# One 512-column matmul in place of two of 256 in the gate/up product of a two-layer decoder trunk

## The chip, the cores and the metric

The kernel runs on one core of a Trainium2 chip, in one launch. The metric is device time in microseconds (us): 1181.53 us is the median of three timed runs of the kernel before (1181.19 to 1183.71).

## The reference

The input is 256 tokens of 1024 features in float32. Two layers follow each other. Each adds half a SwiGLU, then an attention, then half a second SwiGLU to the residual stream. The attention of the first layer is a dilated-window attention, that of the second a latent attention. So there are four SwiGLUs, each with its own weights:

```python
def swiglu(x, w_in, w_out):
    gate, up = jnp.split(x @ w_in, 2, axis=-1)
    return (jax.nn.silu(gate) * up) @ w_out

x = x + 0.5 * swiglu(rmsnorm(x, norm_gains[i, 0]), ffn_w_in[i, 0], ffn_w_out[i, 0])
...                                   # x = x + attention(rmsnorm(x))
x = x + 0.5 * swiglu(rmsnorm(x, norm_gains[i, 2]), ffn_w_in[i, 1], ffn_w_out[i, 1])
```

The hidden width is 2816, that is 22 chunks of 128. The weights are streamed from HBM in pieces of 1 MB.

## The kernel before

Activations stay on the chip with features on the partitions: `xT[p, kt, token]` holds feature kt*128+p of 256 tokens. A float32 product is made of three passes in a rounded 32-bit format (float32r) over an exact split of both operands into a high and a low part: hi·xh + hi·xl + lo·xh, all accumulated in one PSUM bank. The function `mm3` (line 91) issues the three matmuls (lines 95, 96 and 97). The weight is the stationary operand, so each matmul comes with its own weight load, and the 256 tokens are the moving columns.

A weight piece is loaded by SyncE (line 81) into `raw`, cast to `hi` on ScalarE (line 87), and the rest `lo` is taken on VectorE (line 88). Four raw buffers and three each of `hi` and `lo` rotate: a cast waits until the matmuls that read the piece three before it have ended. The gained activation is split in the same way by `split_x` into the tiles `xh` and `xl` (lines 114 and 115), chunk by chunk, at the end of the stage before.

`ffn` (line 170) is a SwiGLU. For each of the 22 hidden chunks c, `up(c)` multiplies by the gate half and the up half of the weights: for each of 8 feature chunks k and for both halves u one `mm3`, 48 matmuls of 256 columns, into the two halves of one PSUM bank of the pool `wk`. `gate(c)` then multiplies the bank by the inverse root mean square of every token (`bc`, line 195, VectorE), applies Silu to the gate half (line 199, ScalarE), multiplies the halves (line 201, VectorE) and splits the product h into `hh` (line 204, ScalarE) and `hl` (line 205, VectorE). `down(c)` multiplies h by 128 rows of the second weight: 24 matmuls of 256 columns into the four accumulator banks of the pool `acc`. The work runs as up, up, two downs, up, up, two downs, where the downs belong to chunks two and three before. The first three ups have no downs between them, because `bc` is not there yet: `stats` and `spread_rstd` (lines 147 and 158) make it with a few small matmuls in the meantime. The last four downs are closed bank by bank (line 247), and each bank's residual and split feed the next stage.

The engines run in order. The order is set at build time: the framework interleaves the instructions of the program by its own estimate of when operands are ready, so an engine's list does not follow the source line by line. Of the eight PSUM banks `acc` has four, `wk` three and `ob` one, for the whole program.

Of the kernel before, what the change touches and what calls it, by code (L numbers as in the profile page):

```python
"""Two-layer hybrid decoder trunk (dilated-window attention, latent attention) on one core.

Activations stay on chip, feature-major: xT[p, kt, token] holds feature kt*128+p.  Products of
float32 operands against the weights run as three float32r passes over an exact split
w = hi + lo (12 significant bits each): hi*xh + hi*xl + lo*xh.  RMS-norm scales are applied
after the products (per token), so a product never waits for a norm's statistics.

The tokens stand even ones first, then odd ones: a dilation of 4 or 16 never joins the two
halves, so those groups' scores are two diagonal blocks.  Only inside the latent layer are they
in their own order, which its input's split and its output's residual turn to and from.  # L10
"""
# [10 lines left out]
F32 = mybir.dt.float32  # L22
# [3 lines left out]
ALU = mybir.AluOpType  # L26
# [24 lines left out]
class Trunk:  # L51
    def __init__(self, ctx, tc):
# [9 lines left out]
        self.wk = e(tc.tile_pool(name="wk", bufs=3, space=PSUM))  # L62
        self.ob = e(tc.tile_pool(name="ob", bufs=1, space=PSUM))
# [3 lines left out]
        self.xh = self.xp.tile([P, KT, S], F32R, name="xh")  # L67
        self.xl = self.xp.tile([P, KT, S], F32R, name="xl")

    # ---- weights: load a piece, split it exactly into two float32r parts  # L70
    def piece(self, src, cuts=1, before=None):
        """cuts: parts the split is made in; before: called ahead of each part's load, else it's one load."""
# [18 lines left out]
    def mm3(self, out, terms, start, stop, **kw):  # L91
        """out += sum over (wh, wl, xh, xl) of w x; the weight is stationary."""
# [6 lines left out]
    # ---- residual stream  # L99
    def split_x(self, d0, xs, in_order=False, shared=False):  # L100
        """Gained x (chunks from d0) as float32r pairs, with the tokens even|odd or in their own order;
        shared: ScalarE and VectorE take turns at the high parts."""
# [14 lines left out]
    def squares(self, d0, xs, in_order=False):  # L117
        """The sum of squares over the chunks."""
# [16 lines left out]
    def residual(self, d0, n, acc, scale, in_order=False):  # L135
        """x += scale * acc for n chunks from d0; acc is their part of a bank, its tokens maybe in order."""
# [10 lines left out]
    def stats(self):  # L147
        """Per-token mean square + eps and its inverse root."""
        nc = self.nc
        ps = self.ob.tile([P, 512], F32, name="ob")  # L150
# [7 lines left out]
    def spread_rstd(self):  # L158
        """The inverse root along the free axis, on every partition."""
# [4 lines left out]
        ps = self.ob.tile([P, 512], F32, name="ob")  # L164
# [4 lines left out]
    # ---- SwiGLU  # L169
    def ffn(self, up_w, out_w, finish, start=None, started=None, hook=None):  # L170
        nc, tc = self.nc, self.tc
        with tc.tile_pool(name="ff", bufs=2) as ff, tc.tile_pool(name="hh", bufs=6) as hp:
            accs = [self.acc.tile([P, 512], F32, name="acc") for _ in range(4)]
            hs, wos = {}, {}

            def up(c, midway=None):
                hi, lo = self.piece(up_w[c], 4 if c < 6 else 1, start if c == 0 else None)
                hv, lv = (t.rearrange("p (k u c) -> p k u c", k=KT, u=2) for t in (hi, lo))
                ps = self.wk.tile([P, 512], F32, name="wk")
                for k in range(KT):  # L180
                    for u in range(2):
                        self.mm3(
                            ps[:, u * S : (u + 1) * S],
                            [(hv[:, k, u, :], lv[:, k, u, :], self.xh[:, k, :], self.xl[:, k, :])],
                            k == 0 and u == 0,
                            k == KT - 1 and u == 1,
                            skip_group_check=True,
                        )
                    if midway and k == KT // 2:
                        midway()  # L190
                return ps

            def gate(c, ps):
                gu = ff.tile([P, 2, S], F32, name="gu")
# [769 lines left out]
```

## Time and profile before

| what | before |
|---|---|
| timed runs, median (range) | 1181.53 us (1181.19 to 1183.71) |
| span of the profiled execution | 1178.2 us |
| TensorE matmul busy (share of the span) | 1159.9 us (98%) |
| VectorE busy | 792.3 us (67%) |
| ScalarE busy | 593.1 us (50%) |
| DMA moved | 196.59 MB, mean 167 GB/s |
| share of the closing chain, by engine | TensorE 90%, VectorE 6% |
| matmuls | 9142, of them 4224 of the gate/up product |

The page of the profile gives for each engine the time in which at least one of its instructions ran. TensorE's matmuls overlap, so a matmul's own duration (0.28 us) is not what it costs: that is the distance from one start to the next. The chain is followed back from the last instruction, at each step to what released it. The profiled execution's own time is its span; the median of the timed runs is 3.3 us longer.

The four SwiGLUs take the stretches 0 to 202, 496 to 686, 686 to 876 and 984 to 1178 us of the span, roughly; the two attentions lie between.

### The profile page before, as it was taken

Reading aid. Unit: us, or ns where it says so; the run is one execution under the profiler, and the core shown is the slowest. Engines: PE = TensorE matmul, PEld = TensorE weight load, DVE = VectorE, ACT = ScalarE, POOL = GpSimd, SP = SyncE. Lnnn points to the kernel's source line nnn. Section 1 sums busy time; section 2 is a strip of 40 time slices with the busy share of each in tenths; the row PEclk is TensorE's granted clock in tenths of the full one; section 3 lists DMA queues with packets and bytes.
Section 4 is the critical chain, followed back from the end, with each engine's and each line's share of the span. In section 5 each row is a group of like instructions: output and inputs, shape, how many; then the busy total and the mean of one; then the engine's idle time right before and its main releaser. Section 6 shows DMA issues by size and latency. Waiting matters only on the chain.

```text
span 1178.2 us, 21736 instructions
## 1 busy us (share of the span) xinstructions
PE 1159.9 (98%) x9142; PEld 1106.9 (94%) x9142; DVE 792.3 (67%) x1384; ACT 593.1 (50%) x980; POOL 102.6 (9%) x98
## 2 busy tenths in 40 slices
PE   7999999999999999999999999999999899999998
PEld 7999999888888888999999999999998789999998
DVE  6855557979777776675555676555576897655554
ACT  6444445556555555654444454444466875444441
POOL 2000001212111111200000020000013212000000
PEclk9999999999999999999999999999999999999999
DMA  8655554554444344155555545555533235455540
GB/s 319 216 182 191 191 186 144 214 179 144 141 146 144 112 158 142 56 215 179 184 184 189 192 182 179 179 179 183 184 129 122 108 110 184 175 183 191 192 149 37
DMA packets 29042, 196.59 MB, mean 167 GB/s; under 512 B 3344, under 2 KB 3856, under 8 KB 5904
## 3 DMA queue, kind: packets, MB, share of 16 engines
q1 hardware_dynamic: 28944, 195.21, 47.4%
q8 instruction: 71, 1.16, 0.4%
q14 instruction: 27, 0.22, 0.1%
HBM read 194.14 MB, written 1.05 MB: 166 GB/s over the span
## 4 chain that ended last, share of the span: by engine, by line
PE 90%; DVE 6%; ACT 2%; issue 1%; POOL 1%; DMA 1%; SPq 0%; DVEq 0%; POOLq 0%
PE wk L96 14%; PE wk L97 14%; PE wk L95 14%; PE acc L95 9%; PE acc L97 9%; PE acc L96 9%; PE acc L418 3%; PE acc L420 3%; PE acc L419 3%; PE wk L358 1%; PE acc L432 1%; PE acc L434 1%; DVE lo L88 1%; PE acc L433 1%; PE ob L491 1%; PE wk L446 1%
## 5 line engine op out<-in xcount | busy, mean ns | idle before, releaser
L88 DVE TENSOR_TENSOR lo<-raw,hi 128x512 fp32r<-128x512 f32 (+2 forms) x408 | 447.0, 1119 | 213.2 <-ACT hi L87 211.6
L87 ACT CAST hi<-raw 128x512 fp32r<-128x512 f32 (+2 forms) x408 | 375.2, 963 | 277.2 <-PE wk L96 172.9
L95 PE MATMUL wk<-xh,hi 128*128 128x256 f32 x1408 | 399.8, 284 | 1.6 <-ACT hi L87 1.6
L97 PE MATMUL wk<-xh,lo 128*128 128x256 f32 x1408 | 399.0, 283 | 1.8 <-DVE lo L88 1.8
L96 PE MATMUL wk<-xl,hi 128*128 128x256 f32 x1408 | 398.8, 283 | 0.1
L97 PEld LDWEIGHTS wk<-xh,lo 128*128 128x128 f32 x1408 | 269.9, 192 | 2.6 <-DVE lo L88 2.6
L95 PEld LDWEIGHTS wk<-xh,hi 128*128 128x128 f32 x1408 | 270.1, 192 | 2.2 <-ACT hi L87 2.1
L96 PEld LDWEIGHTS wk<-xl,hi 128*128 128x128 f32 x1408 | 270.0, 192 | 0.8 <-DVE xl L115 0.5
L95 PE MATMUL acc<-hh,hi 128*128 128x256 f32 x704 | 197.2, 280 | 0.0
L97 PE MATMUL acc<-hh,lo 128*128 128x256 f32 x704 | 196.4, 279 | 0.0
L96 PE MATMUL acc<-hl,hi 128*128 128x256 f32 x704 | 196.4, 279 | 0.0
L95 PEld LDWEIGHTS acc<-hh,hi 128*128 128x128 f32 x704 | 132.3, 188 | 0.0
L97 PEld LDWEIGHTS acc<-hh,lo 128*128 128x128 f32 x704 | 132.3, 188 | 0.0
L96 PEld LDWEIGHTS acc<-hl,hi 128*128 128x128 f32 x704 | 131.9, 187 | 0.0
L204 ACT CAST hh<-h 128x256 fp32r<-128x256 f32 x88 | 35.4, 406 | 168.2 <-DVE h L201 168.0
L195 DVE TENSOR_TENSOR gu<-wk,bc 128x512 f32<-128x512 f32 x88 | 60.5, 691 | 76.5 <-PE wk L97 76.2
L418 PE MATMUL acc<-hi,xh 128*128 128x512 f32 x192 | 76.6, 399 | 0.0
L419 PE MATMUL acc<-lo,xh 128*128 128x512 f32 x192 | 75.2, 392 | 0.0
L420 PE MATMUL acc<-hi,xl 128*128 128x512 f32 x192 | 74.9, 390 | 0.0
L205 DVE TENSOR_TENSOR hl<-h,hh 128x256 fp32r<-128x256 f32 x88 | 37.1, 424 | 33.2 <-ACT hh L204 33.1
L562 POOL TENSOR_TENSOR rr<-r,mhalf 128x8 f32<-128x8 f32 x24 | 39.2, 1636 | 205.2 <-DVE r L560 205.2
L130 POOL TENSOR_TENSOR ssq<-sq 128x256 f32<-128x256 f32 x6 | 4.8, 796 | 596.3 <-ACT sq L127 422.0
(183 smaller groups left out, 1521.3 us busy)
## 6 DMA issues: line engine op xcount, KB each, us to landing
raw<-in_up SPq DMA_DIRECT2D x87, 1024.0 KB, 4.8
raw<-in_down SPq DMA_DIRECT2D x44, 1024.0 KB, 4.8
raw<-in_a_qk SPq DMA_DIRECT2D x24, 1024.0 KB, 4.8
raw<-in_a_v SPq DMA_DIRECT2D x12, 1024.0 KB, 4.8
raw<-in_a_out SPq DMA_DIRECT2D x4, 1024.0 KB, 5.4
raw<-in_b_out SPq DMA_DIRECT2D x4, 1024.0 KB, 4.9
raw<-in_b_in SPq DMA_DIRECT2D x3, 1024.0 KB, 4.9
raw<-in_b_q SPq DMA_DIRECT2D x4, 576.0 KB, 3.6
```

The lines of the kernel that those rows point to most:

```text
L87: nc.scalar.copy(hi[:, c], raw[:, c])
L88: nc.vector.tensor_tensor(lo[:, c], raw[:, c], hi.bitcast(F32)[:, c], op=ALU.subtract)
L95: self.nc.tensor.matmul(out, wh, xh, start=start and i == 0, stop=False, **kw)
L96: self.nc.tensor.matmul(out, wh, xl, start=False, stop=False, **kw)
L97: self.nc.tensor.matmul(out, wl, xh, start=False, stop=stop and i == n - 1, **kw)
L195: nc.vector.tensor_tensor(gu, ps.rearrange("p (u s) -> p u s", u=2), self.bc.unsqueeze(1).broadcast_to([P, 2, S]), op=ALU.mult)
L204: nc.scalar.copy(hh, h)
L205: nc.vector.tensor_tensor(hl, h, hh.bitcast(F32), op=ALU.subtract)
L418: nc.tensor.matmul(pss[tt], xh, hi[:, k, :], start=kk == 0, stop=False)
L419: nc.tensor.matmul(pss[tt], xh, lo[:, k, :], start=False, stop=False)
L420: nc.tensor.matmul(pss[tt], xl, hi[:, k, :], start=False, stop=kk == KT - 1)
L562: nc.gpsimd.tensor_tensor(rr, r8, self.mhalf[:, :8], op=ALU.pow)
```

## The change

In `up` the two parts of the activation now stand side by side in one tile `xs[p, k, part, token]`. The high weight part meets both of them in one matmul of 512 columns, which fills a whole bank: hi·xh in its first half, hi·xl in its second. The low weight part meets `xh` in a matmul of 256 columns that accumulates onto the first half. Gate and up have a bank each, so a chunk takes two banks. Afterwards ScalarE copies the second halves of both banks into SBUF (`rest`), and VectorE adds them to the first halves (`gu`). `gate` then multiplies `gu` by `bc` in SBUF, where before it read PSUM.

The banks are shared out anew: within a SwiGLU a pool `up` has two buffers of two banks each, and `wk` and `ob` exist only within the attentions. The small matmuls of the statistics go to `acc` banks within a SwiGLU, and the accumulators are taken at the first down. Comments were taken out of the file as well, which shifts its line numbers; they are left out here.

```diff
-        self.wk = e(tc.tile_pool(name="wk", bufs=3, space=PSUM))
-        self.ob = e(tc.tile_pool(name="ob", bufs=1, space=PSUM))
...
-        self.xh = self.xp.tile([P, KT, S], F32R, name="xh")
-        self.xl = self.xp.tile([P, KT, S], F32R, name="xl")
+        self.xs = self.xp.tile([P, KT, 2, S], F32R, name="xs")
+        self.xh, self.xl = self.xs[:, :, 0, :], self.xs[:, :, 1, :]
+
+    def attention_banks(self, ctx):
+        self.wk = ctx.enter_context(self.tc.tile_pool(name="wk", bufs=3, space=PSUM, reuse_waits="tile"))
+        self.ob = ctx.enter_context(self.tc.tile_pool(name="ob", bufs=1, space=PSUM, reuse_waits="tile"))
+        self.small = lambda: self.ob.tile([P, 512], F32, name="ob")
...
+            tc.tile_pool(name="up", bufs=2, space=PSUM, reuse_waits="tile") as up_banks,
+        ):
+            self.small = lambda: self.acc.tile([P, 512], F32, name="acc")
+            accs, hs, wos = [], {}, {}
...
-                ps = self.wk.tile([P, 512], F32, name="wk")
+                ps = up_banks.tile([P, 2, 2, S], F32, name="up")
                 for k in range(KT):
+                    both = self.xs[:, k].rearrange("p t s -> p (t s)")
                     for u in range(2):
-                        self.mm3(
-                            ps[:, u * S : (u + 1) * S],
-                            [(hv[:, k, u, :], lv[:, k, u, :], self.xh[:, k, :], self.xl[:, k, :])],
...
+                        nc.tensor.matmul(
+                            ps[:, u].rearrange("p t s -> p (t s)"), hv[:, k, u, :], both, start=k == 0, stop=False, skip_group_check=True
+                        )
+                        nc.tensor.matmul(
+                            ps[:, u, 0, :], lv[:, k, u, :], self.xh[:, k, :], start=False, stop=k == KT - 1, skip_group_check=True
                         )
...
-                return ps
-
-            def gate(c, ps):
-                gu = ff.tile([P, 2, S], F32, name="gu")
-                nc.vector.tensor_tensor(
-                    gu, ps.rearrange("p (u s) -> p u s", u=2), self.bc.unsqueeze(1).broadcast_to([P, 2, S]), op=ALU.mult
-                )
+                rest = ff.tile([P, 2, S], F32, name="rest")
+                nc.scalar.copy(rest, ps[:, :, 1, :])
+                gu = ff.tile([P, 2, S], F32, name="gu", bufs=4)
+                nc.vector.tensor_tensor(gu, ps[:, :, 0, :], rest, op=ALU.add)
+                return gu
+
+            def gate(c, gu):
+                nc.vector.tensor_tensor(gu, gu, self.bc.unsqueeze(1).broadcast_to([P, 2, S]), op=ALU.mult)
...
             def down(c, ds=range(KT)):
                 hi, lo = wos[c // 2]
+                if not accs:
+                    accs.extend(self.acc.tile([P, 512], F32, name="acc") for _ in range(4))
```

The order of instructions moves at three places that matter below. The first is VectorE at the start of the program, from the statistics of the first SwiGLU (`var`) on. Before:

```order
L154 TENSOR_SCALAR var_260<-ob_257 128x2
L163 TENSOR_SCALAR dg_325<-ident_85,rstd_262 128x128 x2
L88 TENSOR_TENSOR lo_217<-raw_214,hi_216 128x512 x4
L167 COPY bc_330<-ob_328 128x256
L195 TENSOR_TENSOR gu_350<-wk_148,bc_330 128x512
```

Now (L159, L168, L172 and L93 are the old lines 154, 163, 167 and 88; L204 is the new add and L208 the multiplication by `bc`):

```order
L159 TENSOR_SCALAR var_230<-acc_227 128x2
L168 TENSOR_SCALAR dg_283<-ident_78,rstd_232 128x128 x2
L204 TENSOR_TENSOR gu_175<-up_140,rest_173 128x512
L172 COPY bc_288<-acc_286 128x256
L93 TENSOR_TENSOR lo_197<-raw_194,hi_196 128x512 x4
L208 TENSOR_TENSOR gu_175<-gu_175,bc_288 128x512
```

The first chunk's add and the copy of `bc` now stand ahead of the split of the second chunk's weights (`lo_217` before, `lo_197` now).

The second is VectorE in the middle of a SwiGLU, over one period of two ups and two downs. Before, `lo_1208` is a piece of the down weights, and the others are of the gate/up weights:

```order
L88 TENSOR_TENSOR lo_1208<-raw_1205,hi_1207 128x2048
L195 TENSOR_TENSOR gu_1195<-wk_1146,bc_330 128x512
L88 TENSOR_TENSOR lo_1273<-raw_1270,hi_1272 128x2048
L201 TENSOR_TENSOR h_1199<-sg_1197,gu_1195 128x256
L205 TENSOR_TENSOR hl_1202<-h_1199,hh_1201 128x256
L195 TENSOR_TENSOR gu_1260<-wk_1211,bc_330 128x512
```

Now, with `lo_1113` a piece of the down weights:

```order
L93 TENSOR_TENSOR lo_1113<-raw_1110,hi_1112 128x2048
L204 TENSOR_TENSOR gu_1047<-up_1012,rest_1045 128x512
L208 TENSOR_TENSOR gu_1047<-gu_1047,bc_288 128x512
L93 TENSOR_TENSOR lo_1167<-raw_1164,hi_1166 128x2048
L212 TENSOR_TENSOR h_1052<-sg_1050,gu_1047 128x256
L204 TENSOR_TENSOR gu_1099<-up_1064,rest_1097 128x512
L216 TENSOR_TENSOR hl_1055<-h_1052,hh_1054 128x256
L208 TENSOR_TENSOR gu_1099<-gu_1099,bc_288 128x512
```

Each chunk has one VectorE instruction more, the add, and `hl` of a chunk now stands behind the add of the next one.

The third is TensorE at the end of the first SwiGLU, where the last chunk's product h meets the down weights. Before, from the 25th matmul after the last up (`hh_2121` is chunk 20, `hh_2186` chunk 21; `acc_109` is the first accumulator):

```order
L95 MATMUL acc_109<-hh_2121,hi_2192 128x256
L96 MATMUL acc_109<-hl_2122,hi_2192 128x256
L97 MATMUL acc_109<-hh_2121,lo_2193 128x256
L95 MATMUL acc_109<-hh_2121,hi_2192 128x256
L96 MATMUL acc_109<-hl_2122,hi_2192 128x256
L97 MATMUL acc_109<-hh_2121,lo_2193 128x256
L95 MATMUL acc_109<-hh_2186,hi_2192 128x256
L96 MATMUL acc_109<-hl_2187,hi_2192 128x256
```

Now, from the 43rd matmul after the last up (`hh_1896` is chunk 21, `hh_1738` chunk 19; `acc_405` is the third accumulator; L100 to L102 are the old lines 95 to 97):

```order
L100 MATMUL acc_405<-hh_1738,hi_1744 128x256
L101 MATMUL acc_405<-hl_1739,hi_1744 128x256
L100 MATMUL acc_403<-hh_1896,hi_1902 128x256
L100 MATMUL acc_404<-hh_1896,hi_1902 128x256
L102 MATMUL acc_405<-hh_1738,lo_1745 128x256
L100 MATMUL acc_405<-hh_1738,hi_1744 128x256
L101 MATMUL acc_403<-hl_1897,hi_1902 128x256
```

The last chunk's `hh` was needed by the 31st matmul after the last up and is now needed by the 45th; its `hl` by the 32nd and now by the 49th. Matmuls of the third accumulator, which before came after the first two were complete, have moved ahead of them.

## Rows read from the trace of the kernel before

**Rows 1.** The page: busy time by engine, and the closing chain by engine.

```profile
PE 1159.9 (98%) x9142; PEld 1106.9 (94%) x9142; DVE 792.3 (67%) x1384; ACT 593.1 (50%) x980; POOL 102.6 (9%) x98
...
PE 90%; DVE 6%; ACT 2%; issue 1%; POOL 1%; DMA 1%; SPq 0%; DVEq 0%; POOLq 0%
```

**Rows 2.** Busy time inside the four SwiGLUs: stretch, length, PE, PEld, DVE, ACT, POOL.

```profile
512.00:683.00 171.00, 171.00 (x1434) 170.95 (x1434) 101.77 (x110) 74.23 (x89) 0.74 (x1) 1.00 0.54 185
...
sum 646.00, PE 646.00 PEld 645.89 DVE 385.40 ACT 277.35 POOL 3.03; mean PE 161.50 PEld 161.47 DVE 96.35 ACT 69.34 POOL 0.76
```

**Rows 3.** Timeline of TensorE, last up to first down: start, duration, line.

```profile
190.58 0.28 PE L95 MATMUL wk<-xh,hi 128*128 128x256 f32 x1
...
190.94 0.28 PE L95 MATMUL acc<-hh,hi 128*128 128x256 f32 x1
...
191.29 0.28 PE L95 MATMUL acc<-hh,hi 128*128 128x256 f32 x1
```

**Rows 4.** Timeline of TensorE in the dilated attention: matmuls of 512 and 256 columns.

```profile
302.59 0.39 PE L418 MATMUL acc<-hi,xh 128*128 128x512 f32 x1
...
306.22 0.39 PE L419 MATMUL acc<-lo,xh 128*128 128x512 f32 x1
...
219.36 0.40 PE L418 MATMUL acc<-hi,xh 128*128 128x512 f32 x1
219.60 0.40 PE L419 MATMUL acc<-lo,xh 128*128 128x512 f32 x1
...
231.18 0.28 PE L432 MATMUL acc<-hi,xh 128*128 128x256 f32 x1
231.29 0.28 PE L433 MATMUL acc<-lo,xh 128*128 128x256 f32 x1
```

**Rows 5.** Groups by line and shape: busy us, mean ns, idle before.

```profile
L360 ACT COPY pt<-wk 128x512 f32<-128x512 f32 x32 | 18.3, 585 | 10.0 <-PE wk L358 10.0
...
L195 DVE TENSOR_TENSOR gu<-wk,bc 128x512 f32<-128x512 f32 x88 | 60.5, 691 | 76.5 <-PE wk L97 76.2
...
L576 DVE TENSOR_TENSOR t<-t,t 128x512 f32<-128x512 f32 x24 | 16.5, 688 | 0.4
...
L88 DVE TENSOR_TENSOR lo<-raw,hi 128x2048 fp32r<-128x2048 f32 x108 | 247.5, 2292 | 149.6 <-ACT hi L87 149.5
```

**Rows 6.** Timeline at the second chunk of the first SwiGLU: VectorE, then TensorE.

```profile
17.91 0.48 DVE L163 TENSOR_SCALAR dg<-ident,rstd 128x128 f32<-128x128 f32 x2 [0.83 <-POOL rstd L156]
18.31 2.49 DVE L88 TENSOR_TENSOR lo<-raw,hi 128x512 fp32r<-128x512 f32 x4
...
18.54 0.67 PE L165 MATMUL ob<-dg,ones 128*128 128x256 f32 x2 [1.65 <-DVE dg L163]
...
19.28 0.28 PE L97 MATMUL wk<-xh,lo 128*128 128x256 f32 x1
```

**Rows 7.** Timeline at the entry to the second SwiGLU: VectorE, then TensorE.

```profile
499.70 1.83 DVE L115 SCALAR_TENSOR_TENSOR xl<-xg,xh 128x256 fp32r<-128x256 f32 x2
...
500.71 0.39 PE L96 MATMUL wk<-xl,hi 128*128 128x256 f32 x1
...
501.58 0.39 PE L96 MATMUL wk<-xl,hi 128*128 128x256 f32 x1
```

**Rows 8.** Timeline at the end of the first SwiGLU: VectorE, ScalarE, TensorE.

```profile
191.14 0.69 DVE L195 TENSOR_TENSOR gu<-wk,bc 128x512 f32<-128x512 f32 x1 [0.37 <-PE wk L97]
191.75 1.28 DVE L88 TENSOR_TENSOR lo<-raw,hi 128x512 fp32r<-128x512 f32 x2
...
193.89 0.42 DVE L205 TENSOR_TENSOR hl<-h,hh 128x256 fp32r<-128x256 f32 x1
...
191.06 1.14 ACT L87 CAST hi<-raw 128x512 fp32r<-128x512 f32 x2 [0.75 <-PE wk L96]
192.11 0.42 ACT L199 ACTIVATE sg<-gu 128x256 f32<-128x256 f32 x1
...
194.47 0.28 PE L95 MATMUL acc<-hh,hi 128*128 128x256 f32 x1
```

More of the change, by code (lines that the diff above doesn't have):

```diff
@@ L149, in stats @@
         nc = self.nc
-        ps = self.ob.tile([P, 512], F32, name="ob")
+        ps = self.small()
         for tt in range(NTT):
@@ L163, in spread_rstd @@
             nc.vector.tensor_scalar(dg[:, tt, :], self.ident, self.rstd[:, tt : tt + 1], None, op0=ALU.mult)
-        ps = self.ob.tile([P, 512], F32, name="ob")
+        ps = self.small()
         nc.tensor.matmul(ps[:, :S], self.ones, dg.rearrange("p t s -> p (t s)"), start=True, stop=True)
@@ L171, in ffn @@
         nc, tc = self.nc, self.tc
-        with tc.tile_pool(name="ff", bufs=2) as ff, tc.tile_pool(name="hh", bufs=6) as hp:
-            accs = [self.acc.tile([P, 512], F32, name="acc") for _ in range(4)]
-            hs, wos = {}, {}
+        with (
+            tc.tile_pool(name="ff", bufs=2) as ff,
+            tc.tile_pool(name="hh", bufs=6) as hp,
+            tc.tile_pool(name="up", bufs=2, space=PSUM, reuse_waits="tile") as up_banks,
+        ):
+            self.small = lambda: self.acc.tile([P, 512], F32, name="acc")
+            accs, hs, wos = [], {}, {}
             def up(c, midway=None):
@@ L178, in up @@
                 hv, lv = (t.rearrange("p (k u c) -> p k u c", k=KT, u=2) for t in (hi, lo))
-                ps = self.wk.tile([P, 512], F32, name="wk")
+                ps = up_banks.tile([P, 2, 2, S], F32, name="up")
                 for k in range(KT):
+                    both = self.xs[:, k].rearrange("p t s -> p (t s)")
                     for u in range(2):
-                        self.mm3(
-                            ps[:, u * S : (u + 1) * S],
-                            [(hv[:, k, u, :], lv[:, k, u, :], self.xh[:, k, :], self.xl[:, k, :])],
-                            k == 0 and u == 0,
-                            k == KT - 1 and u == 1,
-                            skip_group_check=True,
+                        nc.tensor.matmul(
[3 more added lines that the diff above has]
+                            ps[:, u, 0, :], lv[:, k, u, :], self.xh[:, k, :], start=False, stop=k == KT - 1, skip_group_check=True
                         )
@@ L268, in setup_first @@
         nc.scalar.activation(self.st.tile([P, 2], F32, name="warm"), self.mhalf[:, :2], AF.Silu)
-        ps = self.ob.tile([P, 512], F32, name="ob")
+        ps = self.acc.tile([P, 512], F32, name="acc")
         for _ in range(10):
@@ L393, in dilated @@
         with (
+            ExitStack() as banks,
             tc.tile_pool(name="at", bufs=2) as at,
@@ L396, in dilated @@
         ):
+            self.attention_banks(banks)
             oth = ot.tile([P, KT, S], F32R, name="oth")
@@ L588, in latent @@
         with (
+            ExitStack() as banks,
             tc.tile_pool(name="la", bufs=2) as la,
@@ L591, in latent @@
         ):
+            self.attention_banks(banks)
             oth = lb.tile([P, KT, S], F32R, name="oth")
```

## The prediction

> **What bounds the kernel now.** I read the page first. TensorE has a matmul running in 98% of the span, and 90% of the closing chain is TensorE [rows 1]. The table of stretches then shows that inside the four SwiGLUs this is not 98% but all of it: 646.00 us of 646, with VectorE at 385 us (60%) and ScalarE at 277 us (43%), at the full granted clock of 2.4 GHz [rows 2]. So in these stretches only what shortens TensorE's list, or stops it, moves the end. What a matmul costs there is read from the timeline as the distance between starts: three matmuls of the gate/up product stand 0.36 us apart (190.58 to 190.94), 120 ns each; three of the down product take 0.35, some 118 each [rows 3]. The busy time of 0.28 us per matmul is overlap and no price.
>
> **The merged matmul.** For each of 22 chunks, 8 feature chunks, 2 halves and 4 SwiGLUs, 1408 times, three matmuls of 256 columns (360 ns) become one of 512 and one of 256. The gate/up product never runs 512 columns, but the dilated attention does, with the same float32r operands and a weight load for each matmul: from 302.59 to 306.22 lie 16 steps, 227 ns each [rows 4]. Twice 256 columns cost 240 there, so the second 256 columns add 107 ns and each separate matmul about 13 ns on top of its columns. Merging two saves those 13 ns.
>
> No row shows the two widths in turn all the time; changes of width are there singly. The 512 that comes first after 256s takes 0.24 (219.36 to 219.60), and the 256 that comes first after 512s takes 0.11 (231.18 to 231.29) [rows 4]. The bounds are thus 227 + 110 = 337 ns (saving 23 ns, 32 us in all) and 240 + 120 = 360 ns (saving nothing). I take 347: it is what the steady rates give (227 + 120), and the two odd ones together (240 + 110 = 350) lie beside it. Saving: 13 ns x 1408 = 18.3 us.
>
> The Trainium skill, on the page "TensorE: Matmul & The Clock Gate", section "Wait — 56ns, not 53.3ns?", states that a warm matmul costs its columns at 2.4 GHz plus about 2.5 ns, whatever its length. By that figure merging saves 2.5 ns x 1408 = 3.5 us, an estimate from that page, and the waits below would leave 1.4 us of it. The trace differs: 120 ns for 256 columns is 13 above their time, and 512 columns are 13 above theirs as well [rows 3, 4]. The measurement decides, and I keep 13.
>
> **The evacuation.** Each of 88 chunks gets a ScalarE copy of 128x512 from PSUM and a VectorE add of the same size. The nearest rows are the copy `pt<-wk` at 585 ns, and 691 ns for the product out of PSUM that the add replaces there; the multiplication by `bc`, now out of SBUF, is like `t<-t,t` at 688 [rows 5]. That is 51 us more for ScalarE and 61 us more for VectorE. In the stretches of rows 2 some 75 of the 88 chunks run (646 us at 8.6 a chunk: 48 x 120 ns and 24 x 118), so VectorE goes from 385 to about 437 of 646 us and ScalarE from 277 to about 321. Neither becomes the bound, and TensorE's own work hides both as long as three hand-overs hold:
>
> Banks in the loop. `up` has two buffers, so up(c+2) waits for the add of c. Between the end of up(c) and the start of up(c+2) lie one up (16 x 347 = 5.55 us) and two downs (48 x 118 = 5.65), 11.2 us; copy and add take 0.6 + 0.7, so about 9.7 us are left. What stands ahead of the add in VectorE's list is the split of a down piece, 2.29 us [rows 5]. Its cast (four times the 0.52 us that a quarter takes, 191.06 to 192.11 for two [rows 8]) waits for the downs to end, so the split is over some 4.4 us after them and up(c) ends only 5.55 us after them. Cost zero; if the cover were gone it would be a wait in each of 40 periods.
>
> Banks at the start of a SwiGLU. There up0, up1 and up2 follow each other, and up2 needs up0's banks. Up0's add stands behind a cast and a split of a down piece: 2.1 for the cast, then the copy (0.6) beside the split, to about 4.4 us, then the add to 5.1 us after up0's end. Up1 and the statistics take 5.55 + 0.3. Zero, with 0.7 us to spare, at three starts.
>
> The last chunk's h. Before, with T = 190.94 (the first down after the last up), the product with `bc` starts at T + 0.20 and `hl` is ready at 193.89 + 0.42, T + 3.4; the down that wants `hh` starts at 194.47, T + 3.5 [rows 8]. Nothing was to spare. Now the chain is copy to T + 0.8, add to 1.55, on VectorE a quarter split and `hl` of chunk 20 before the multiplication (ends at 3.1), Silu behind two casts to 3.6, h to 4.1, `hh` to 4.55, and `hl` behind one more quarter split to 5.0 (durations as in rows 8; instructions of an engine follow each other closer than they last, 0.52 for a ScalarE cast of 512 and 0.61 for a VectorE op). In the old order of matmuls TensorE would stand still for some 1.4 us at each of four ends. But the order has moved: `hh` of the last chunk is wanted by the 45th matmul (44 x 118 = T + 5.2) and `hl` by the 49th (T + 5.65). Zero, with 0.6 us to spare; 5.6 us if that cover fails.
>
> **What it does cost.** At the start of the program the second chunk's `lo` moves behind the add and behind `bc`. `dg` ends at 18.39; the add follows from 18.31 to 19.0; `bc` waits for the matmul pair that ends at 18.54 + 0.67 = 19.21 and takes about 0.4 (as `hl`, the same size, in rows 8); the first quarter of `lo` (2.49 / 4, 0.6 to 0.7) ends near 20.3. TensorE wanted it at 19.28 [rows 6]: 1.0 us. Queued behind it are the other quarters, which stay ahead of TensorE (0.62 each against 1.39 us of matmuls), and the same chain costs an estimated 0.3 us again at the fourth chunk. Together 1.3.
>
> At the entries to the second and the fourth SwiGLU (one is shown) TensorE waits for `xl` of the last two feature chunks, at 500.71 and 501.58, right as VectorE ends them (499.70 + 1.83) [rows 7]. The end of that first chunk is set by VectorE, so its saving (16 x 13 = 0.2) is lost, and the hi·xh pass that used to run ahead of the wait is now part of the wide matmul behind it (0.1): 0.3 each, 0.6. The program's first chunk is paced by its loads and splits: 0.2.
>
> Sum against the profiled execution: 1178.2 - 18.3 + 1.3 + 0.6 + 0.2 = 1162.0 us of span. The median of the timed runs lies 3.3 us above that span, so 1165.3.
>
> **Rivals.**
> The covers fail. VectorE and ScalarE are fuller, the spare times are 0.6 and 0.7 us, and they rest on an order made from estimates. Four ends at 1.4 and three starts at 0.7 give 7.7 us back: 1173. For it speaks that nothing was to spare before [rows 8]; against it the moved order.
>
> The change of width costs. If every 512 behind a 256 takes 0.25 rather than the 0.24 seen at the first one, a merged pair costs 370 ns, 10 more than the three: 14 us more plus the 2.1 of waits, 1197.6, slower. Place: each of 1408 wide matmuls. It decides from 238 ns per wide matmul on, where the saving falls below the 2.1 us of waits. For it speaks the 0.24; against it the 0.11 of the return and that later ones fall to 227 [rows 4].
>
> Hardly anything is saved. If a merged pair saves only the 2.5 ns of the fixed part that the page named above gives, the time is 1181.5 - 3.5 + 2.1 = 1180.1, no change. As a mechanism here: the 13 ns would belong to each 256 columns and not to the matmul. Rows 4 speak against it, since 512 columns carry them once.
>
> It gains more. If the new layout of `xs` brings the gate/up matmuls to the rate of the downs (118 instead of 120 [rows 3], and so 2 to 2.5 ns less on each of 2 x 1408), another 6 us go: 1159. No row says that it does: what makes the 2 ns is not to be seen.
>
> **How the numbers follow.** The forecast with small shifts of the waits (1162.5 to 1168.5) gets 0.63; covers fail 0.18 (1168.5 to 1175); more gain 0.09; hardly anything saved 0.05; change of width 0.05. The predicted time is 1165.3. The range from 1160.5 to 1174 takes in the forecast and nearly all of the failing covers, and leaves out most of the last three, about 0.17. A measurement of this kernel tells 0.2% (2.4 us) from no change. The first three cases are faster by more than that: 0.90. The fourth is no change, 0.05, and the fifth slower, 0.05.
>
> **What would show it.** In the middle of a SwiGLU a wide and a narrow matmul together should take 0.347 us, and a period of two ups and two downs 16.75 us instead of 17.17. TensorE should still show no idle time there, and the group of the add no wait that TensorE takes over. Around 19 us a wait for `lo` of 1 us should stand in TensorE's timeline, and none after the last up of a SwiGLU. The prediction is wrong if the pair takes more than 355 ns, or if TensorE waits for `gu` or `hh` in every period.

## The result and the profile after

| | before | after |
|---|---|---|
| timed runs, median (range) | 1181.36 us (1179.39 to 1183.71, 4 runs) | 1169.81 us (1168.45 to 1173.94, 4 runs) |
| span of the profiled execution | 1178.2 us | 1166.6 us |
| predicted | | 1165.3 us (1160.5 to 1174) |

The ratio is 0.9907 (95% interval 0.9885 to 0.9929): faster by 11.5 us where 16.2 were forecast. The page of the kernel after, busy time, chain by engine, and five of its groups (busy us, mean ns, idle before):

```profile
PE 1147.2 (98%) x7734; PEld 1029.5 (88%) x7734; DVE 840.2 (72%) x1472; ACT 635.0 (54%) x1068; POOL 103.5 (9%) x98
...
PE 87%; DVE 7%; ACT 2%; issue 2%; POOL 1%; DMA 0%; SPq 0%; DVEq 0%; POOLq 0%; ACTq 0%
...
L193 PE MATMUL up<-xs,hi 128*128 128x512 f32 x1408 | 496.9, 397 | 1.4 <-ACT hi L92 0.8
L196 PE MATMUL up<-xs,lo 128*128 128x256 f32 x1408 | 393.9, 280 | 2.9 <-DVE lo L93 2.9
...
L204 DVE TENSOR_TENSOR gu<-up,rest 128x512 f32<-128x512 f32 x88 | 60.3, 685 | 5.1 <-ACT rest L202 4.8
L208 DVE TENSOR_TENSOR gu<-gu,bc 128x512 f32<-128x512 f32 x88 | 60.4, 689 | 1.4
L202 ACT COPY rest<-up 128x512 f32<-128x512 f32 x88 | 50.3, 571 | 11.8 <-PE up L196 11.8
```

Against [rows 1] TensorE has 1408 matmuls fewer and is still the engine that sets the time. The new copy and add cost 571 and 685 ns, as the rows chosen for them said (585, 691 [rows 5]). The table of stretches inside the four SwiGLUs (columns as in [rows 2]) shows whether they are hidden:

```profile
sum 636.00, PE 636.00 PEld 580.86 DVE 421.60 ACT 312.05 POOL 0.00; mean PE 159.00 PEld 145.22 DVE 105.40 ACT 78.01 POOL 0.00
```

TensorE has no idle time there, with VectorE at 66% and ScalarE at 49% (68% and 50% were worked out). So the cover in the loop held, and a pair's price is again the distance between starts. In the first SwiGLU, TensorE's timeline of the kernel after:

```profile
99.72 0.40 PE L193 MATMUL up<-xs,hi 128*128 128x512 f32 x1
99.95 0.28 PE L196 MATMUL up<-xs,lo 128*128 128x256 f32 x1
100.07 0.39 PE L193 MATMUL up<-xs,hi 128*128 128x512 f32 x1
...
100.76 0.39 PE L193 MATMUL up<-xs,hi 128*128 128x512 f32 x1
```

Three pairs take 1.04 us, 347 ns each, as forecast. But the same lines in the second SwiGLU read:

```profile
549.69 0.40 PE L193 MATMUL up<-xs,hi 128*128 128x512 f32 x1
549.93 0.28 PE L196 MATMUL up<-xs,lo 128*128 128x256 f32 x1
550.04 0.40 PE L193 MATMUL up<-xs,hi 128*128 128x512 f32 x1
...
550.75 0.40 PE L193 MATMUL up<-xs,hi 128*128 128x512 f32 x1
```

Here three pairs take 1.06 us, 353 ns each (over seven periods of two ups and two downs: 118.67 us against 117.32, and 120.26 before). The second place that differs is the second chunk of the program, in TensorE's timeline:

```profile
17.44 0.70 PE L170 MATMUL acc<-dg,ones 128*128 128x256 f32 x2 [1.56 <-DVE dg L168]
17.79 0.58 PE L193 MATMUL up<-xs,hi 128*128 128x512 f32 x1
19.26 0.58 PE L196 MATMUL up<-xs,lo 128*128 128x256 f32 x1 [0.89 <-DVE lo L93]
19.64 0.63 PE L193 MATMUL up<-xs,hi 128*128 128x512 f32 x1
20.07 0.42 PE L196 MATMUL up<-xs,lo 128*128 128x256 f32 x1
20.28 0.63 PE L193 MATMUL up<-xs,hi 128*128 128x512 f32 x1
```

The first narrow matmul stands 1.47 us behind its wide one, and the pairs after it 0.64 us apart. The stretches of the same kernel say why (columns as in [rows 2]; the third number from the end is the granted clock):

```profile
17.40:18.85 1.45, 0.93 (x3) 0.49 (x3) 1.26 (x3) 1.45 (x4) 0.00 (x0) 1.00 0.93 395
18.85:22.20 3.35, 2.94 (x10) 2.56 (x10) 3.35 (x7) 2.02 (x5) 0.00 (x0) 0.50 0.31 56
```

The wait for `lo` is there, 0.89 us for 1.0 forecast (against none in [rows 6]). What was not forecast is the clock: 0.50, the level of 1.2 GHz, from 18.85 to 22.2 us. The chunk took 8.27 us; by the forecast (16 pairs at 347 ns, the wait of 1.0 and the small matmul ahead) it would have been 6.7.

The third place is the end of a SwiGLU, where [rows 8] stand for before. ScalarE, then TensorE, of the kernel after (T, the first down after the last up, is 188.03):

```profile
188.15 0.62 ACT L92 CAST hi<-raw 128x512 fp32r<-128x512 f32 x1 [3.16 <-issue]
188.68 0.41 ACT L210 ACTIVATE sg<-gu 128x256 f32<-128x256 f32 x1
189.00 0.56 ACT L202 COPY rest<-up 128x512 f32<-128x512 f32 x1
...
190.86 0.52 PE L100 MATMUL acc<-hh,hi 128*128 128x256 f32 x3
191.42 0.39 PE L101 MATMUL acc<-hl,hi 128*128 128x256 f32 x1
```

A cast of the next stage's weights stands ahead of chunk 20's Silu. It starts right behind the last wide matmul of the last up (187.68 + 0.40), as the cast of [rows 8] did: at the end of a SwiGLU two of the three buffers hold the last down pieces, so the cast waits for the piece of chunk 21 and not, as it would be with the piece three before, for chunk 20's. `hl` of chunk 20 is late, and TensorE starts no matmul between 191.09 and 191.42. The same cast stands ahead of chunk 21's copy, which ends at T + 1.5, and chunk 21's `hh` comes at T + 5.35:

```profile
192.97 0.41 ACT L215 CAST hh<-h 128x256 fp32r<-128x256 f32 x1 [0.49 <-DVE h L212]
```

At the fourth end, which has no next stage, TensorE waits for `hh` of chunk 21 itself (T is 1150.64):

```profile
1154.90 0.50 PE L100 MATMUL acc<-hh,hi 128*128 128x256 f32 x2 [0.20 <-ACT hh L215]
```

From T to the last down the four ends took 11.55, 11.55, 11.55 and 11.76 us; 11.19 each before.

### The profile page after: what moved, and what is told of

It reads as the page before. It is cut to its first block, busy times and chain, and to the rows that moved or that the text cites. A ratio compares the mean times of both kernels' runs of the same rounds, so it can differ in the third digit from the quotient of the medians.

```text
span 1166.6 us, 19188 instructions
## 1 busy us (share of the span) xinstructions
PE 1147.2 (98%) x7734; PEld 1029.5 (88%) x7734; DVE 840.2 (72%) x1472; ACT 635.0 (54%) x1068; POOL 103.5 (9%) x98
## 4 chain that ended last, share of the span: by engine, by line
PE 87%; DVE 7%; ACT 2%; issue 2%; POOL 1%; DMA 0%; SPq 0%; DVEq 0%; POOLq 0%; ACTq 0%
PE up L193 27%; PE up L196 13%; PE acc L100 9%; PE acc L101 9%; PE acc L102 8%; PE acc L433 3%; PE acc L435 3%; PE acc L434 3%; DVE lo L93 2%; PE wk L371 2%; PE acc L447 2%; PE acc L449 1%; PE acc L448 1%; ACT hi L92 1%; PE ob L506 1%
## 5 line engine op out<-in xcount | busy, mean ns | idle before, releaser
L93 DVE TENSOR_TENSOR lo<-raw,hi 128x512 fp32r<-128x512 f32 (+2 forms) x408 | 447.5, 1120 | 245.6 <-ACT hi L92 245.3
L193 PE MATMUL up<-xs,hi 128*128 128x512 f32 x1408 | 496.9, 397 | 1.4 <-ACT hi L92 0.8
L196 PE MATMUL up<-xs,lo 128*128 128x256 f32 x1408 | 393.9, 280 | 2.9 <-DVE lo L93 2.9
L193 PEld LDWEIGHTS up<-xs,hi 128*128 128x128 f32 x1408 | 265.2, 188 | 63.6 <-DVE xs L120 1.9
L196 PEld LDWEIGHTS up<-xs,lo 128*128 128x128 f32 x1408 | 265.9, 189 | 4.7 <-DVE lo L93 4.6
L102 PE MATMUL acc<-hh,lo 128*128 128x256 f32 x704 | 196.2, 280 | 0.0
L100 PE MATMUL acc<-hh,hi 128*128 128x256 f32 x704 | 195.5, 280 | 0.2 <-ACT hh L215 0.2
L100 PEld LDWEIGHTS acc<-hh,hi 128*128 128x128 f32 x704 | 131.6, 188 | 2.1 <-ACT hh L215 0.4
L102 PEld LDWEIGHTS acc<-hh,lo 128*128 128x128 f32 x704 | 132.3, 188 | 0.0
L433 PE MATMUL acc<-hi,xs 128*128 128x512 f32 x192 | 76.7, 399 | 0.0
L434 PE MATMUL acc<-lo,xs 128*128 128x512 f32 x192 | 75.3, 392 | 0.0
L435 PE MATMUL acc<-hi,xs 128*128 128x512 f32 x192 | 75.0, 391 | 0.0
L204 DVE TENSOR_TENSOR gu<-up,rest 128x512 f32<-128x512 f32 x88 | 60.3, 685 | 5.1 <-ACT rest L202 4.8
L208 DVE TENSOR_TENSOR gu<-gu,bc 128x512 f32<-128x512 f32 x88 | 60.4, 689 | 1.4
L202 ACT COPY rest<-up 128x512 f32<-128x512 f32 x88 | 50.3, 571 | 11.8 <-PE up L196 11.8
L447 PE MATMUL acc<-hi,xs 128*128 128x256 f32 x192 | 55.4, 288 | 0.0
```

The lines of the kernel that those rows point to most:

```text
L93: nc.vector.tensor_tensor(lo[:, c], raw[:, c], hi.bitcast(F32)[:, c], op=ALU.subtract)
L100: self.nc.tensor.matmul(out, wh, xh, start=start and i == 0, stop=False, **kw)
L102: self.nc.tensor.matmul(out, wl, xh, start=False, stop=stop and i == n - 1, **kw)
L193: nc.tensor.matmul(ps[:, u].rearrange("p t s -> p (t s)"), hv[:, k, u, :], both, start=k == 0, stop=False, skip_group_check=True)
L196: nc.tensor.matmul(ps[:, u, 0, :], lv[:, k, u, :], self.xh[:, k, :], start=False, stop=k == KT - 1, skip_group_check=True)
L208: nc.vector.tensor_tensor(gu, gu, self.bc.unsqueeze(1).broadcast_to([P, 2, S]), op=ALU.mult)
```

## The experiments

**The merge alone.** The high weight part met xh and xl in two matmuls again:

```diff
-  nc.tensor.matmul(ps[:, u].rearrange("p t s -> p (t s)"), hv[:, k, u, :], both, start=k == 0, ...)
+  nc.tensor.matmul(ps[:, u, 0, :], hv[:, k, u, :], self.xh[:, k, :], start=k == 0, ...)
+  nc.tensor.matmul(ps[:, u, 1, :], hv[:, k, u, :], self.xl[:, k, :], start=False, ...)
```

> Only the merge is undone: the high weight part meets xh and xl in two matmuls of 256 columns, written to the two halves of the same bank; banks, the copy and the add stay as in the changed kernel. Theory (the merge pays 13 ns on each of 1408 pairs, and the evacuation, the order of the work and the clock take some 7 us of it back): 1169.8 + 18.3 = 1188 us, some 7 us above the kernel before; two gate/up chunks and two down chunks take 17.18 us again in all four SwiGLUs. Rival (the gain came from the new banks and the earlier start, the merge itself pays little): 1170 to 1176 us, and the period stays near 16.8 us.

Measured: 1183.03 us, ratio to before 1.0015 (1.0006 to 1.0025; below, too, the first number in brackets is the ratio to the kernel before, and the others are its 95% interval). TensorE in the middle of its first SwiGLU, three matmuls to 0.36 us:

```profile
100.72 0.28 PE L193 MATMUL up<-xs,hi 128*128 128x256 f32 x1
...
101.08 0.28 PE L193 MATMUL up<-xs,hi 128*128 128x256 f32 x1
```

All four SwiGLUs are back at 17.18 us a period, so the whole gain is the merge's. The evacuation and the new order without it cost 2.6 us (2.1 were forecast, in part at other places). That run shows the slow second chunk (7.96 us) and long ends (11.50, and 11.33 at the fourth) as well, so neither comes from the wide matmul. The expected size was missed: the merge is worth 13.2 us against the first measurement of the kernel after and 10.5 against a second one below, not 18.3.

**The clock and the wait at the second chunk.** First the order alone, in the first SwiGLU:

```diff
+  with tc.issue_after(self.cast.ins), tc.issue_after(self.sub.ins):   # chunk 1's last cast and lo
+      p0 = early()                                                    # chunk 0's copy and add
...
+  with self.tc.issue_after(self.after):                               # chunk 1's last lo
+      nc.vector.tensor_copy(self.bc, ps[:, :S])
```

> In the first SwiGLU alone, chunk 0's copy (ScalarE) stands behind chunk 1's four casts, and its add (VectorE) behind chunk 1's four low parts, so that TensorE does not wait for them. Theory (VectorE's low part stood behind the add and the copy of bc, that wait of 0.89 us is what halved TensorE's clock, and both go together): the second chunk takes 5.6 to 6.0 us instead of 8.27, granted clock 1.00 from 17.8 to 23 us, total 2.3 us less, 1167.5 us. Rival 1 (the clock falls in any case, because TensorE was idle before it from 15.9 to 17.4 us): only the wait goes, second chunk 7.4 us, 1168.9 us. Rival 2 (the bank of chunk 0 comes free too late): the third chunk waits what the second gains, 1169.8 us.

Measured: 1172.34 us (0.9922, 0.9907 to 0.9936). Rival 1: the wait was gone, the clock fell nonetheless, and the chunk took 7.37 us. The stretches of that run:

```profile
17.90:18.20 0.30, 0.20 (x1) 0.20 (x2) 0.30 (x2) 0.30 (x2) 0.00 (x0) 1.00 1.16 437
18.20:22.10 3.90, 3.90 (x14) 3.29 (x14) 3.90 (x8) 2.40 (x3) 0.00 (x0) 0.57 0.46 139
```

So my first reading, that the 0.89 us of waiting halved the clock, fell. Next, work for TensorE in its empty time before the chunk, without and with the order:

```diff
+  pf = self.small()
+  with self.tc.issue_after(last.ins):                                 # the statistics' matmul
+      for _ in range(3):
+          nc.tensor.matmul(pf[:, :P], self.ones, self.ones, start=True, stop=True)
```

> The changed kernel with three matmuls of 128 columns on constants (0.43 us each in the warm-up at the start, 1.28 us) put into TensorE's empty time after the first chunk, from 15.9 to 17.4 us; their result is not used. Theory (the clock was halved from 18.9 us on because TensorE had too little to do before, whatever it waited for then): granted clock 1.00 from 18 to 23 us, the second chunk 6.8 us instead of 8.27 with the wait for its low part still there, 1.5 us less. Rival (the wait of 0.89 us at 18.4 us is what halves it): 8.3 us as before. The total is this and what the pattern of matmul starts does, which changed from 347 to 353 ns a pair in two more SwiGLUs of the run with the low parts first, at 1.6 us each: 1168.3 us if the pattern stays, up to 1171.5 us if not.

> The three filling matmuls together with chunk 0's copy and add behind chunk 1's casts and low parts. Theory (clock and wait are two losses with two causes): both go, the second chunk takes 5.6 to 6.0 us at a granted clock of 1.00, 2.4 us less than in the changed kernel. Rival (the clock falls for something else, such as the load of the first 15 us): 7.4 us as with the low parts first alone, and a clock of 0.50 again. Total 1167.4 us with the pattern of the changed kernel, up to 1171 us where more SwiGLUs fall into 353 ns a pair.

Measured: 1171.1 us (0.9912, 0.9897 to 0.9927) and 1170.64 us (0.9907, 0.9892 to 0.9921). With the filling alone the wait is still 0.88 us, and the clock stays up; the chunk takes 6.90 us. With both it takes 5.73. In the trace the three matmuls are six instructions of 0.91 us together (1.28 were expected), and they cut the empty time from 1.56 to 0.78 us. The stretches with the filling alone:

```profile
17.30:19.30 2.00, 1.22 (x9) 1.03 (x9) 0.96 (x4) 2.00 (x5) 0.71 (x1) 1.00 0.91 356
19.30:26.00 6.70, 5.82 (x33) 4.79 (x33) 6.51 (x13) 4.84 (x8) 0.00 (x0) 1.00 0.44 152
```

And the chunk with both edits, at 1.00 as well:

```profile
18.40:24.50 6.10, 6.03 (x34) 5.30 (x35) 6.10 (x12) 2.69 (x3) 0.00 (x0) 1.00 0.62 220
```

So the filling keeps the clock, and the wait does not take it. In this pair of runs the clock costs 1.4 us (8.27 to 6.90) and the wait 1.2 (6.90 to 5.73). The other profiles bear it out: all five with the filling (two here, three below) stay at 1.00 there, and all eight without it, of the kernel after and its variants, fall to 0.50. In three of the eight the clock is low for 3.4 us, in four for 6.8, in one for 6.8 and again 3.4. The second profile of the unaltered kernel (below) is one of the four; its clock fell between 16.70 and 16.80 us, in the empty time, before the second chunk had started (18.60):

```profile
16.80:23.50 6.70, 4.87 (x13) 3.68 (x14) 5.38 (x11) 4.85 (x10) 0.57 (x1) 0.50 0.46 152
```

Its second chunk took 8.65 us, and those of the other three 8.91 to 9.30, so the 1.4 us is the least that the clock cost. In the one profile of the kernel before the clock stayed at 1.00 behind an empty time as long (1.65 us [rows 6]):

```profile
18.50:24.50 6.00, 5.96 (x48) 5.94 (x49) 5.97 (x11) 2.31 (x3) 0.00 (x0) 1.00 0.64 232
```

The run without the merge, with the matmuls of before and the wait for `lo`, lost the clock, and so did the low parts first, with fewer matmuls and no wait. Why the kernel before kept it, and whether it does so in every execution, is not shown.

The totals of these two runs and of the low parts first are not below the first measurement of the kernel after (1169.81 us), for two reasons. The low parts first bring a new wait for a low part at some 50 us, in the sixth chunk (the seventh starts 0.5 us late), and there is the next point.

**The two rates.** In these runs the third and fourth SwiGLU had gone to 353 ns a pair as well. Three runs looked for what sets it. The address of `xs`:

```diff
+        self.xp.tile([P, 16], F32, name="pad")
         self.xs = self.xp.tile([P, KT, 2, S], F32R, name="xs")
```

> The tile with xh and xl starts 64 bytes further on in its partition, nothing else is changed. Down matmuls, whose h tiles start at such an address, take 117.7 ns, gate/up matmuls of 256 columns took 120 in the kernel before, where x's tiles start at a multiple of 256 bytes. Theory 1 (the address of the moving operand sets these 2 to 3 ns, and the patterns): some 342 ns a pair in all four SwiGLUs, 1162 us, and the second SwiGLU as fast as the others. Theory 2 (the difference comes from elsewhere): 347 or 353 ns as before, 1169.8 us give or take 1.6 us for each SwiGLU that changes its pattern.

Measured: 1170.27 us (0.9901, 0.9887 to 0.9916), at 347, 353, 347, 347 ns: the address of `xs` is not it. The kernel after once more:

> The changed kernel once more, unaltered. Theory (which of the two patterns of starts a SwiGLU falls into is settled anew in each execution, by the times at which its first chunks start): the profile shows 347 and 353 ns a pair in another distribution over the second to fourth SwiGLU than the first profile did (353, 347, 347), the first stays at 347, and the times of the executions lie 0 to 3.2 us above 1168.4. Rival (the pattern belongs to the kernel's own order of instructions): 353, 347, 347 again. The start of the second chunk differs by up to 1.5 us from 17.8 us, as the loads at the start land.

Measured: 1172.57 us (0.9924, 0.9912 to 0.9937). The same kernel, and its profile has 347, 353, 353, 353 ns (seven periods 117.32, 118.67, 118.67, 118.67 us). TensorE in its third SwiGLU:

```profile
749.91 0.40 PE L193 MATMUL up<-xs,hi 128*128 128x512 f32 x1
...
750.97 0.40 PE L193 MATMUL up<-xs,hi 128*128 128x512 f32 x1
```

So the rate is settled in each execution. The first chunks of a SwiGLU can run at either rate; from the seventh at the latest it keeps one, through 250 pairs or more with downs in between. The second SwiGLU was at 353 in all eight profiles with this order of matmuls, the first at 347, and the last two at either (353 in five and in six of the eight). The times lie 3.0 to 4.7 us above 1168.4, more than expected. The profile is 4.4 us longer than the first one: 3.5 in the loops of the two SwiGLUs that changed their rate, and 1.3 at the program's start, where the second chunk started at 18.60 us, 0.8 later, and the clock was low for twice as long. Last, the order of widths:

```diff
                     for u in range(2):
                         nc.tensor.matmul(ps[:, u]..., hv[:, k, u, :], both, ...)       # wide
+                    for u in range(2):
                         nc.tensor.matmul(ps[:, u, 0, :], lv[:, k, u, :], self.xh[:, k, :], ...)  # narrow
```

> Order inside a gate/up chunk: gate wide, up wide, gate narrow, up narrow, instead of wide and narrow in turn; the same matmuls, the same sums. Theory (a matmul costs its columns and some ns of its own, whatever stands beside it, and the slower second SwiGLU is a pattern of starts that depends on the turn): 347 ns a pair in all four SwiGLUs, the second one loses its 353 ns, 1.5 to 2 us less, 1168 us. Rival 1 (each change of width costs): half as many changes, some 5 ns less on each of 1408 pairs, 1162 us. Rival 2 (the second SwiGLU is slow for what its data or its place bring): 1169.8 us, its period still 16.95 us.

Measured: 1169.17 us (0.9895, 0.9878 to 0.9911). All four SwiGLUs run at 16.81 us a period, 349 ns a pair, here and in three later profiles (where the wait in the sixth chunk adds 0.5 us to one period). So rival 1 fell (half as many changes of width save nothing), and the slow pattern belongs to the strict turn of widths. The steady rate is 2 ns above the 347 expected. TensorE in the third SwiGLU (a row is two matmuls):

```profile
750.02 0.63 PE L193 MATMUL up<-xs,hi 128*128 128x512 f32 x2
750.49 0.39 PE L197 MATMUL up<-xs,lo 128*128 128x256 f32 x2
750.71 0.63 PE L193 MATMUL up<-xs,hi 128*128 128x512 f32 x2
```

**The ends.** A first edit held the next casts behind the last chunk's cast of h, but the cast that it caught was that of the last down piece.

> The next stage's first casts on ScalarE stand behind the last gate/up chunk's cast of h, instead of ahead of the last two chunks' Silu. Theory (the cast waits for a weight buffer until the last gate/up matmul, and holds up the Silu of chunk 20 and the copy of chunk 21 behind it): from the first down matmul of the end to the last 11.2 us instead of 11.55 in the first three SwiGLUs, the fourth stays at 11.76; 1.1 us less, 1168.7 us. Rival (the down products wait for the longer way of the last chunk, copy, add and multiplication, whatever stands ahead of it): ends stay at 11.5 us, 1169.8 us. Other side (the held casts make the next stage start late): entries longer by up to 1 us each, 1171 to 1173 us.

Measured: 1181.41 us (1.0006, 0.9996 to 1.0015), ends of 12.59 us, with TensorE waiting 0.6 us for that piece's low part; it tells nothing of the theory. The ends are 4 of the 12 us lost. Casts held that late cost more: the two attentions took 1.3 and 1.7 us longer than in the first profile of the kernel after, and the first chunk of the third SwiGLU 2.0. The edit in its right place:

```diff
+  if pair == NC_FF // 2 - 1:
+      self.pin = self.last_rest              # chunk 21's copy on ScalarE
...
+  with self.tc.issue_after(self.pin) if self.pin else ExitStack():
       nc.scalar.copy(hi[:, c], raw[:, c])    # the next piece's four casts
```

> The next stage's first four casts stand behind the last chunk's copy (instead of one ahead of chunk 20's Silu), and the last down piece's cast is left where it was. Theory (that cast held up chunk 20's Silu by 0.6 us, and TensorE waited 0.33 us for chunk 20's low part): no wait after the last gate/up matmul, 11.2 us for the end of the first three SwiGLUs instead of 11.55; the fourth, which has no next stage, stays at 11.76. Rival (the copy and the add make the last two chunks late by themselves): 11.5 us as before. Total 1168.7 us, if no SwiGLU changes its pattern.

Measured: 1175.54 us (0.9946, 0.993 to 0.9963), ends of 11.68, 11.58, 11.32 and 11.66 us. The wait for chunk 20 was gone, and TensorE waited for chunk 21 instead (194.32 to 194.81):

```profile
194.32 0.28 PE L104 MATMUL acc<-hl,hi 128*128 128x256 f32 x1
194.81 0.51 PE L103 MATMUL acc<-hh,hi 128*128 128x256 f32 x2 [0.21 <-ACT hh L218]
```

The held casts cost more elsewhere: the first chunk of the third SwiGLU took 6.72 us for 5.71, the latent attention 109.2 for 107.9. Then the three edits above together, the same with the last two chunks copied, added and multiplied in halves, and that with the casts held behind the last cast of h:

```diff
+  halves = lambda c: (slice(0, 1), slice(1, 2)) if c >= NC_FF - 2 else (slice(0, 2),)
+  for h in halves(c):
+      nc.scalar.copy(rest[:, h], ps[:, h, 1, :])
+      nc.vector.tensor_tensor(gu[:, h], ps[:, h, 0, :], rest[:, h], op=ALU.add)
```

> Three edits that were run apart or in pairs: filling matmuls, low parts first, and the order gate wide, up wide, gate narrow, up narrow. Theory (the clock's loss and the pattern's loss are separate and add up): second chunk 5.6 to 5.8 us, 16.81 us for two gate/up and two down chunks in all four SwiGLUs, ends 11.55 as before: 1167.4 - 3.2 = 1164.2 us in span, 1167 us measured. Rival (the order with two wide ones was steady by chance in its one profile): some SwiGLU at 16.95 or 16.75, 1166 to 1171 us.

> As the run with the three edits, and the last two gate/up chunks of each SwiGLU are copied, added and multiplied in halves, gate first, so that Silu starts a half earlier. Theory (TensorE waits at the end for the longer way of the last two chunks, 0.33 us in the first three SwiGLUs and 0.48 in the fourth): ends 11.2 us in all four, 1.6 us less than without it, 1162.6 us in span. Rival (the next stage's cast on ScalarE still stands ahead of the last chunk's copy and makes it late): ends 11.3 to 11.6, the same time as without.

> As the run with the split end, and the next stage's first four casts stand behind the last chunk's cast of h, so that nothing of the next stage stands between the last two chunks' steps on ScalarE and VectorE. Theory (what is late at the end is the longer way of the last two chunks plus the next stage's steps in between; with both gone the cover of the prediction holds): no wait after the last gate/up matmul in the first three SwiGLUs, 11.2 us for their ends instead of 11.54; the fourth stays at 11.4. Rival (the halved steps are themselves too long for the last chunk): 11.4 us in all four. What the held casts cost at the start of the next stages decides the total: 1166 us measured if they are hidden behind the 11 us of down products, up to 1172 us if they push the next stage's first low parts behind its residual and split.

Measured: the three edits 1166.83 us (0.9876, 0.9861 to 0.9892), 5.7 us below the second measurement of the kernel after: second chunk 5.76 us, 16.81 us in all SwiGLUs but for that one period, ends of 11.55 and a fourth of 11.75, as the theory had it. With halves 1167.02 (0.9879, 0.9866 to 0.9893), the same: the ends with a next stage stay at 11.54, only the fourth falls to 11.40. With halves and held casts 1168.84 (0.9902, 0.9886 to 0.9919), ends of 11.69, 11.68, 11.41 and 11.96. VectorE at its first end (T = 186.38), where nothing of the next stage stands in between:

```profile
187.16 0.42 DVE L226 TENSOR_TENSOR gu<-up,rest 128x256 f32<-128x256 f32 x1
187.62 0.43 DVE L233 TENSOR_TENSOR gu<-gu,bc 128x256 f32<-128x256 f32 x1
187.96 0.42 DVE L241 TENSOR_TENSOR hl<-h,hh 128x256 fp32r<-128x256 f32 x1
188.29 0.42 DVE L226 TENSOR_TENSOR gu<-up,rest 128x256 f32<-128x256 f32 x1
188.75 0.43 DVE L233 TENSOR_TENSOR gu<-gu,bc 128x256 f32<-128x256 f32 x1
189.28 0.43 DVE L237 TENSOR_TENSOR h<-sg,gu 128x256 f32<-128x256 f32 x1
```

These steps follow each other with hardly a gap. The two ends of the way on ScalarE are:

```profile
186.63 0.37 ACT L225 COPY rest<-up 128x256 f32<-128x256 f32 x1 [0.27 <-PE up L216]
...
189.74 0.41 ACT L240 CAST hh<-h 128x256 fp32r<-128x256 f32 x1 [1.18 <-DVE h L237]
```

From the copy to `hh` it takes 3.5 us, `hh` stands at T + 3.8, and TensorE's order has it next at T + 3.5 and waits till 190.19. Neither side came as it was stated: three of the ends are longer than the rival's 11.4 too. The edit moved the downs again, `hh` of the last chunk being the 31st matmul's operand here and the 45th's (T + 5.2) in the kernel after. The first run that held the casts in the right place had it at the 39th. By the order of the kernel after, T + 3.8 would have been in time with 1.4 us to spare. In each of these runs the new order left the chunk less time than its way takes. Whether the last chunk would be in time with the casts away and the order kept was not run.

## Why the prediction was right, and where it was short

The mechanism was right: the merge is the whole gain, 347 ns for a pair is what the first SwiGLU takes, the period is the 16.75 us named, and the loop and the banks hide copy and add. The 360 ns of "nothing saved" and the 370 of "change of width costs" are out, and so is the rate of the downs (some 342 ns a pair) of "it gains more". The Trainium skill's page "TensorE: Matmul & The Clock Gate", section "Wait — 56ns, not 53.3ns?", gives a fixed 2.5 ns a matmul, which would make the merge worth 3.5 us, an estimate from that figure. The run without the merge puts it at 10.5 to 13.2, so the measurement stands against the page here.

Stage by stage, in the two profiled executions, the span fell by 11.6 us where 16.2 were forecast:

| stage | forecast | measured |
|---|---|---|
| program start to the first gate/up matmul | 0 | -0.43 |
| loops, chunk 4 to the last up, four SwiGLUs | -15.0 | -13.4 |
| chunks 0 to 3, first SwiGLU | +0.7 | +1.3 |
| chunks 0 to 3, the other three | -1.9 | -0.9 |
| four ends | 0 | +1.65 |
| attentions | 0 | +0.1 |

**"Saving: 13 ns x 1408".** The size holds for three loops of that execution (3.78 us less each, 13.1 ns a pair) and is 7.1 ns in the second, 2.04 us. The first chunks of the second to fourth SwiGLU run at 353 ns in good part too, which is most of the 1.0 us missing there. In the second profile of the kernel three SwiGLUs ran at 353, and their loops took 3.5 us more: the term is 13 ns for the first SwiGLU, 7 for the second, and 7 or 13 for the last two, as it falls.

**"At the start of the program: 1.3".** The wait was 0.89 us and the estimated second one at the fourth chunk did not come. What the step left out is the clock, 1.4 us or more, which the rows of before could not show, since it did not fall there in that profile. The early start (-0.43) and a first chunk faster by 0.64 us are luck of that execution: loads landed early (ScalarE's second weight cast, which a load released in both, started at 7.80 us for 8.77), and in ten of the twelve experiments the second chunk started 0.5 us or more behind that of the first profile. Without this 1.1 us the forecast would have been missed by more.

**"At the entries: 0.3 each"** held: the first chunks of the second and fourth SwiGLU took 6.32 and 6.35 us (6.21 and 6.22 before).

**"The last chunk's h: zero, with 0.6 us to spare".** This step failed: 0.36 us at three ends and 0.57 at the fourth. It put Silu of chunk 21 behind two casts but did not ask what a cast does to chunk 20, though the `[0.75 <-PE wk L96]` in [rows 8] showed that such a cast waits for the last up. The copy of chunk 21, worked out to end at T + 0.8, stands behind that cast too and ended at T + 1.5, so that `hl` came at T + 5.85 for 5.0, and the order wanted it at T + 5.65; the wait for chunk 20 hid most of that. For the fourth end the step took over the order of the first, but there `hh` is wanted by the 34th matmul, at T + 3.9, and stood at T + 4.2. The rival "covers fail" priced an end at 1.4 us; 0.36 to 0.57 came.

**"Banks at the start of a SwiGLU: zero, 0.7 to spare"** held at all three. So did the banks in the loop (11.2 less 1.3 leaves 9.9 us there, not 9.7).

What stays open is what the 347 and 353 ns are made of, and why the second SwiGLU always falls to the slower one. That the address of `xs` does not set it, that it changes between executions, and that two wide matmuls in a row end it, is shown; the mechanism is not.

## What to carry to other kernels

Where matmuls are TensorE's whole time, count them as well as their columns: one matmul fewer was worth 7 to 13 ns here, and the extra work on the other engines was free inside the loop and paid for at the seams. At each seam follow the last chunk through the new steps, and also what the next stage has put into the same engine's list. A short empty time of TensorE that cost nothing in the profile before went with a halved clock in every profile of the changed kernel that left it empty; three small matmuls put into it kept the clock and shortened the chunk behind it by 1.4 us.

## What the hardware showed beside this

A stream of 512- and 256-column matmuls in turn, each with its own weights, has two steady rates, 347 and 353 ns a pair, and one execution can hold both; in the order wide, wide, narrow, narrow it has one, 349. TensorE's clock was granted at 0.50 for 3.4 or 6.8 us (in one run for both, one after the other) near an empty time of 1.56 us at the program's start, in all eight profiles of the kernel after and its variants that left it empty, with a wait for `lo` behind it and without. With 0.91 us of small matmuls in the same place it stayed at 1.00 in all five, in one of them in spite of a wait of 0.88 us.
